# The last four halves of a norm's modulation as multiply-adds on VectorE, the norm chain in front, and fillers on TensorE at the beginning

## The chip, the cores and the metric

One core of a Trainium2 chip runs one layer of a decoder. The metric is device time in microseconds (us) of one execution. The kernel before takes 649.06 us (median of 3 runs, 648.49 to 649.7). The engines are TensorE (PE, with its weight loads PEld), VectorE (DVE), ScalarE (ACT), GpSimd (POOL) and the queue SP, which issues the transfers of the weights.

## The reference, cut to what matters

```python
def rms_norm(x, g):
    y = xf * lax.rsqrt(jnp.mean(xf * xf, axis=-1, keepdims=True) + NORM_EPS)
    return y * g

def modulate(x, g, shift, scale):
    return rms_norm(x, g) * (1.0 + scale[:, None, :]) + shift[:, None, :]

mod = jax.nn.silu(c) @ w_ada[l] + b_ada[l]          # 1 x 6144, from 1024 x 6144 weights
sh1, sc1, g1, sh2, sc2, g2 = jnp.split(mod, 6, axis=-1)
h = modulate(x, norm1_g[l], sh1, sc1)               # 256 x 1024
proj = h @ w_in[l]                                  # 1024 x 3592
...
```

After that come block attention, an mLSTM, an output projection with the gate g1, a second modulated norm (sh2, sc2), a mixture of 32 experts (the routing picks two per token) and a last norm. All is in float32. The change touches only how `sc1` and `sh1` are computed, and the order of the work around them.

## The kernel before, in words

The 256 tokens lie as two tiles of 128. `xt` holds x with tokens on the partitions; TensorE transposes it (`transpose2`, L309) and VectorE and ScalarE copy it out as `xT`, eight blocks k of 128 channels by 256 tokens (`x_evac`, L323). All weights come through a ring of 23 slots of 1 MB (`issue`, `fill`, L135 to L170): SP issues the next chunk when a slot is free, in the order of the list `order`; `done()` gives a slot back, `big()` takes one for a work tile.

The first norm has two parts. `norm1_scale` (L339 to L344) makes 1/rms per token from the sums of squares that ScalarE took; `norm1_rows` (L346) spreads it over the partitions with a matmul as `R1`. The modulation is the product of silu(c) with `w_ada`. Its first 2048 columns (`sh1`: blocks j = 0, 1; `sc1`: blocks j = 2, 3) are used in eight halves of 256 columns, one 1 MB chunk each. `ada_half(j, h)` (L398) computes one half on TensorE, in 8 matmuls with c as the stationary side (L404; the records count 16, two passes each), and VectorE copies the row out of PSUM (L408). `ada_half_cols` (L411) turns it into columns by two tiny matmuls and VectorE adds the bias (L416). Then `mod_a1` (L457) makes (1 + scale) * g, `mod_scale` (L462) multiplies two blocks of `xT` by it and by `R1` on VectorE, and `mod_shift` (L466, L467) adds the shift on ScalarE: once as `hh`, rounded to the matmul's 32-bit form, once back into `xT`. `mod_lo` (L470) makes the rest `hl` = xT - hh on VectorE.

So blocks k = 2m and 2m+1 of h need the halves m of `sc1` and `sh1`, and the loop over m = 0, 1, 2 (L512 on) is a pipeline: in step m TensorE multiplies blocks 2m and 2m+1 with the weights of k, q and v (six calls of `ip`, L489, n = 0 to 5), while the halves for step m+1 are made between them, at n = 2 and n = 4. Each `ip` needs its 128 x 512 weights as a rounded part `whb` (ScalarE, L210) and a rest `wlb` (GpSimd, L211), made by `split_to` into four buffers each, at most three calls ahead; ScalarE may fill a buffer again when TensorE is done with it. I call one such pair of instructions a split.

In all this part each instruction is pinned: `P(...)` and `behind` tie it to the one written before it on its engine, so that the order on an engine is the order of the code. Behind the loop the framework orders the instructions by its own plan. There `mac` (L384) already makes blocks j = 4, 5 and 6 of the modulation on VectorE, one multiply-add per 128 rows of weights, 512 columns wide (L364, L366).

The tile `rowb` holds small parameters, among them the inverse frequencies of the rotary angles (`invf`), which `rope_angles` (L271) reads; ScalarE's queue issues its transfer at the start (L180). `rope_angles` runs in step m = 0 on VectorE, with two sines on ScalarE (L280, L284).

## Time and profile before

| | before |
|---|---|
| median of 3 runs | 649.06 us |
| the profiled execution | 649.01 us |
| its span in the profile | 647.4 us |
| mean granted clock of TensorE | 0.973 of full speed |
| PE, DVE, ACT, POOL busy | 563.3, 170.2, 144.0, 103.7 us |
| weights and data moved | 248.31 MB, mean 384 GB/s |

The span is cut into 40 slices of 16.2 us on the page; a row of digits gives the busy tenths of an engine, PEclk the granted clock in tenths of full speed, GB/s what the transfers moved. Times in the rows below are microseconds from the span's start. A pair "start us, us" is the start and the length; neighbouring instructions of a kind are merged into one row with their count. An idle time in square brackets is that of the engine ahead of the row, with what ended it.

### The profile page before, as it was taken

The page shows a single profiled execution, that of the slowest core. Times are in us where ns is not written, and L with a number is a line of the kernel's source. Part 1 is how long each engine was busy: PE and PEld are TensorE (multiplying, and loading weights), DVE is VectorE, ACT ScalarE, POOL GpSimd, SP SyncE. Part 2 cuts the span into 40 slices and gives each one's busy share as a digit, 9 for nine tenths or more (in the row PEclk, how much of TensorE's full clock was granted, in tenths as well). Part 3 has the DMA queues.
Part 4 walks back from the last instruction along what each step waited for, and adds up shares of the span by engine and source line. Part 5 has one row for each costly group of instructions (what it writes and reads, how often), then busy time and mean ns, then how long its engine had stood idle before and what let it go on. Part 6 is the DMA issues. An engine that isn't in the chain of part 4 may idle for free.

```text
span 647.4 us, 7994 instructions
## 1 busy us (share of the span) xinstructions
PE 563.3 (87%) x3178; PEld 275.3 (43%) x3178; DVE 170.2 (26%) x448; ACT 144.0 (22%) x306; POOL 103.7 (16%) x98
## 2 busy tenths in 40 slices
PE   4899989999997999998889869877988798889874
PEld 3576878875685444352123214211421332233122
DVE  1533979852745030220002002000100110100013
ACT  5453567854443110000000000000000000001013
POOL 2566746672630000000000000000000000000000
PEclk9799999998996999999989999998999999999998
DMA  8999963699696899999999999999999999999994
GB/s 339 423 425 425 415 264 103 245 353 377 220 403 251 330 427 427 427 425 425 428 428 427 425 427 427 429 426 426 426 428 427 426 425 428 425 426 426 428 383 148
DMA packets 41640, 248.31 MB, mean 384 GB/s; under 512 B 4352, under 2 KB 10624, under 8 KB 12928
## 3 DMA queue, kind: packets, MB, share of 16 engines
q1 hardware_dynamic: 41024, 247.00, 92.5%
q10 hardware_dynamic: 576, 0.76, 0.3%
q8 instruction: 26, 0.43, 0.2%
q14 instruction: 14, 0.11, 0.1%
HBM read 246.70 MB, written 1.05 MB: 383 GB/s over the span
## 4 chain that ended last, share of the span: by engine, by line
DMA 50%; PE 36%; DVE 8%; ACT 2%; SPq 2%; issue 1%; DVEq 0%; ACTq 0%
DMA we<-in_wexp_dram 49%; PE f L1124 4%; PE f1a L1103 3%; PE f1b L1103 3%; PE xg_ps L1024 2%; SPq L156 2%; PE adap L404 1%; PE acc L1136 1%; DVE rowb L366 1%; PE xg_ps L1038 1%; DMA xt<-in_x_dram 1%; DVE ropd L563 1%; PE s_ps L637 1%; PE pk L494 1%; PE pk L495 1%
## 5 line engine op out<-in xcount | busy, mean ns | idle before, releaser
L1103 PE MATMUL f1a<-we,xgt 128*32 128x512 f32 x512 | 134.1, 605 | 30.2 <-DMA we<-in_wexp_dram 30.2
L1103 PE MATMUL f1b<-we,xgt 128*32 128x512 f32 x512 | 133.0, 594 | 0.0
L1124 PE MATMUL f<-we,htb 128*32 128x512 f32 (+2 forms) x576 | 82.8, 572 | 17.3 <-DMA we<-in_wexp_dram 17.3
L211 POOL TENSOR_TENSOR wlb<-wi,whb 128x512 fp32r<-128x512 f32 x56 | 74.6, 1349 | 56.4 <-ACT whb L210 48.8
L1103 PEld LDWEIGHTS f1a<-we,xgt 128*32 128x32 f32 x512 | 23.9, 109 | 105.0 <-DMA we<-in_wexp_dram 81.0
L1103 PEld LDWEIGHTS f1b<-we,xgt 128*32 128x32 f32 x512 | 32.7, 109 | 72.6 <-issue 69.8
L1109 ACT ACTIVATE sab<-f1a 128x256 f32<-128x256 f32 x8 | 3.1, 384 | 247.0 <-PE f1a L1103 247.0
L1110 DVE TENSOR_TENSOR acb<-sab,f1a 128x256 f32<-128x256 f32 x8 | 3.4, 422 | 202.6 <-ACT sab L1109 202.6
L1124 PEld LDWEIGHTS f<-we,htb 128*32 128x32 f32 x576 | 21.2, 113 | 64.9 <-DMA we<-in_wexp_dram 31.6
L210 ACT ACTIVATE whb<-wi 128x512 fp32r<-128x512 f32 x56 | 34.5, 632 | 26.8 <-PE pv L497 7.6
L1130 DVE TENSOR_TENSOR ysb<-f,g2b 128x512 f32<-128x512 f32 (+2 forms) x18 | 11.4, 632 | 93.1 <-PE f L1124 93.1
L1024 PEld LDWEIGHTS xg_ps<-gsb,xt 128*128 128x128 f32 x224 | 26.7, 191 | 13.3 <-issue 7.9
L1029 ACT ACTIVATE xgt<-xg_ps,modc,a 128x128 f32<-128x128 f32 x28 | 10.5, 457 | 93.2 <-PE xg_ps L1024 93.2
L1024 PE MATMUL xg_ps<-gsb,xt 128*128 128x128 f32 x224 | 28.6, 279 | 1.9 <-ACT xgt L1029 1.9
L1136 PE MATMUL acc<-ysb,pwb 128*128 128x512 f32 x56 | 27.3, 613 | 2.5 <-DVE ysb L1130 2.3
L211 POOL TENSOR_TENSOR wlb<-wo,whb 128x512 fp32r<-128x512 f32 x16 | 21.0, 1317 | 23.7 <-ACT whb L210 23.2
L366 DVE SCALAR_TENSOR_TENSOR rowb<-wa,cs,rowb 128x512 f32<-128x512 f32 x21 | 23.9, 1139 | 0.3
L506 PE MATMUL pc<-hl,whb 128*128 128x256 f32 x64 | 18.4, 289 | 0.0
L505 PE MATMUL pc<-hh,whb 128*128 128x256 f32 x64 | 18.2, 286 | 0.0
L1136 PEld LDWEIGHTS acc<-ysb,pwb 128*128 128x128 f32 x56 | 9.6, 189 | 19.2 <-issue 8.9
L507 PE MATMUL pc<-hh,wlb 128*128 128x256 f32 x64 | 17.7, 289 | 0.0
L1012 DVE TENSOR_TENSOR gsb<-iot,posm 128x128 f32<-128x128 f32 x16 | 4.4, 289 | 35.7 <-PE xg_ps L1024 32.1
(371 smaller groups left out, 691.5 us busy)
## 6 DMA issues: line engine op xcount, KB each, us to landing
we<-in_wexp_dram SPq DMA_DIRECT2D x188, 1024.0 KB, 19.6
wa<-in_wada_dram SPq DMA_DIRECT2D x24, 1024.0 KB, 13.6
wi<-in_win_dram SPq DMA_DIRECT2D x8, 1024.0 KB, 18.4
wi<-in_win_dram SPq DMA_DIRECT2D x12, 512.0 KB, 14.0
wo<-in_wout_dram SPq DMA_DIRECT2D x4, 1024.0 KB, 7.2
we<-in_wexp_dram SPq DMA_DIRECT2D x4, 512.0 KB, 16.8
we<-in_wexp_dram SPq DMA_DIRECT2D x8, 256.0 KB, 6.3
xt<-in_x_dram SPq DMA_DIRECT2D x1, 1024.0 KB, 5.7
```

What stands on the lines that cost most here:

```text
L156: behind(nc.sync.dma_start(chunks[key][:, 4 * c:4 * (c + n)].rearrange("p (f n) -> p f n", f=4), src[:, :, c:c + n]))
L210: P(A.activation(hi, src, AF.Copy))
L211: G.tensor_tensor(lo, src, hi.bitcast(F32), OP.subtract)
L366: i = V.scalar_tensor_tensor(r, w, cs[:, k:k + 1], r, op0=OP.mult, op1=OP.add)
L505: T.matmul(o, wh[:, cc], hh[:, k], start=k == 0 and c % 2 == 0, stop=False)
L506: T.matmul(o, wh[:, cc], hl[:, k], start=False, stop=False)
L507: T.matmul(o, wl[:, cc], hh[:, k], start=False, stop=k == 7 and c % 2 == 1)
L1024: T.matmul(p[:, (k % 4) * 128:(k % 4 + 1) * 128], xn[:, t, k * 128:(k + 1) * 128], gsb[:, q % 2, t], start=t == 0, stop=t == 1)
L1103: T.matmul(hid[h][CAP * i:CAP * (i + 1), :], xgb[q % 2][:, k, i * CAP:(i + 1) * CAP], w[:, h * 512:(h + 1) * 512], start=k == 0, stop=k == 7)
L1124: m = T.matmul(py[CAP * i:CAP * (i + 1), 0:n], htb[:, f // 2, o:o + CAP], chunks["e", 3 * (4 * q + i) + 2, dh][:, w0:w0 + n], start=f == 0 ...
L1130: V.tensor_tensor(ysb[q % 2][:, c0:c0 + n], py[:, 0:n], g2b[:, c0:c0 + n], OP.mult)
L1136: T.matmul(acc[b], pwb[:, q % 2, t * 128:(t + 1) * 128], ysb[q % 2][:, h * 512:(h + 1) * 512], start=q == 0, stop=q == NQ - 1 - h)
```

## The change

Four things change. The last four halves, for steps m = 1 and m = 2 (`sc1` and `sh1`, halves 2 and 3 of four), are no longer made by TensorE: `ada_half_mac` makes each of them on VectorE in 8 multiply-adds of 256 columns (one TENSOR_SCALAR, seven SCALAR_TENSOR_TENSOR that add to their own result), 4 at each of n = 0 to 3; `ada_mac_cols` turns the row into columns with two tiny matmuls against ones, at n = 4 and n = 5. The halves for step m = 1, made in step m = 0, stay on TensorE. `norm1_scale` moves ahead of the second copy of `xT` and of the first half's copy, and the last two copies of `xT` (on ScalarE) move behind the first `mod_shift`. Of the first splits two instead of three stand ahead of `mod_shift`. TensorE gets transposes of the identity into an unused bank: 28 ahead of x's transposes, then 4, 4 and 8 between the first halves. The transfer of `rowb` moves from ScalarE's queue to SP's, behind the first five chunks.

```diff
@@ -29,6 +29,7 @@
 MLS = (0, 1, 2, 3)
 CT = (3, 5)
 PIN = 24
+WARM = 28
 MACS = (1, 1, 0, 0)
 SLOTS = 23
 KEEP = 9
@@ -120,6 +121,8 @@
         ins = i.ins
         prev = next((x for x in reversed(nc.cur_bb.bb.instructions)
                      if x is not ins and x.engine == ins.engine and x.name not in floating), None)
+        if prev is None:
+            return
         tc.add_manual_dep(ins, prev.name, mybir.DependencyInfo(mybir.DependencyClass.NoSync,
                                                                mybir.DependencyReason.DATA), reason="order")
 
@@ -133,6 +136,8 @@
     keep = [KEEP]
 
     def issue():
+        if nissued[0] == 5:
+            behind(nc.sync.dma_start(rowb[:, 1536:1996], colp[:, 96:556]))
         kind, j, h = order[nissued[0]][:3]
         part = order[nissued[0]][3:]
         if part == (1,):
@@ -177,7 +182,6 @@
 
     nc.sync.dma_start(xt, x.rearrange("(t p) d -> p t d", p=128))
     rowb = big("rowb", [128, 2048])
-    nc.scalar.dma_start(rowb[:, 1536:1996], colp[:, 96:556])
     convw = rowb[:, 1536:1568].rearrange("p (i c) -> p i c", i=4)
     wgate = rowb[:, 1568:1632].rearrange("p (k n) -> p k n", k=8)
     wr = rowb[:, 1632:1920].rearrange("p (k n) -> p k n", k=8)
@@ -314,6 +318,13 @@
     hh = big("hh", [128, 8, S], F32R)
     hl = big("hl", [128, 8, S], F32R)
     pinned[0] = True
+    wp = pA("warm")
+
+    def fillers(n):
+        for _ in range(n):
+            P(T.transpose(wp[:, 0:128], ident, ident))
+
+    fillers(WARM)
     xps = [pacc(f"tp{kk}") for kk in range(4)]
     for kk in range(4):
         transpose2(xt, kk, xps[kk])
@@ -415,6 +426,29 @@
         c0 = 4 * j + 2 * h
         P(V.tensor_tensor(modc[:, c0:c0 + 2], p[:, 256:258], bada[:, c0:c0 + 2], OP.add))
 
+    def ada_half_mac(j, h):
+        r = arow(256)
+        w = chunks["a", j, h].rearrange("p (k n) -> p k n", k=8)
+
+        def run(ks):
+            for k in ks:
+                if k == 0:
+                    P(V.tensor_scalar(r, w[:, k], cs[:, 0:1], None, op0=OP.mult))
+                else:
+                    P(V.scalar_tensor_tensor(r, w[:, k], cs[:, k:k + 1], r, op0=OP.mult, op1=OP.add))
+            if 7 in ks:
+                done()
+
+        return j, h, r, run
+
+    def ada_mac_cols(half):
+        j, h, r, _ = half
+        p = psm("adap")
+        for b in range(2):
+            P(T.matmul(p[:, b:b + 1], r[:, b * 128:(b + 1) * 128], ones[:, 0:1], start=True, stop=True))
+        c0 = 4 * j + 2 * h
+        P(V.tensor_tensor(modc[:, c0:c0 + 2], p[:, 0:2], bada[:, c0:c0 + 2], OP.add))
+
     late = []
 
     def late_rows(j):
@@ -471,19 +505,22 @@
 
     G.memset(wg32, 0.0)
     x_evac(V, 0)
+    norm1_scale()
     x_evac(V, 1)
-    x_evac(A, 2)
-    x_evac(A, 3)
     half = ada_half(2, 0)
-    norm1_scale()
+    fillers(4)
     norm1_rows()
     ada_half_cols(half)
     mod_a1(0)
     half = ada_half(0, 0)
-    ahead()
+    fillers(4)
     mod_scale(0)
+    split_to(2)
     ada_half_cols(half)
+    fillers(8)
     mod_shift(0)
+    x_evac(A, 2)
+    x_evac(A, 3)
 
 
     def ip(p, j, k):
@@ -518,6 +555,21 @@
             rope_tables()
             P(V.tensor_copy(wg32[:, :, 0:8], wgate))
         for n in range(6):
+            if m > 0:
+                if n in (0, 2):
+                    hm = ada_half_mac(2 + j if n == 0 else j, h)
+                    if n == 0:
+                        hs_ = hm
+                if n < 4:
+                    hm[3](range(4 * (n % 2), 4 * (n % 2) + 4))
+                if n == 4:
+                    ada_mac_cols(hs_)
+                    mod_a1(m + 1)
+                    mod_scale(m + 1)
+                if n == 5:
+                    ada_mac_cols(hm)
+                ip((pk, pq, pv)[n // 2], (1, 0, 2)[n // 2], 2 * m + n % 2)
+                continue
             if n == 2:
                 half = ada_half(2 + j, h)
             if n == 4:
```

The order on VectorE around step m = 1 (tile names as in the code: `hl` the rests, `rowb` the row of a half, `wa_0_93` and `wa_0_97` the chunks of a half, `a` the factor, `R` is `R1`). Before:

```order
L470 TENSOR_TENSOR hl<-xT,hh 128x256 x2
L408 COPY rowb<-adap 128x256
L416 TENSOR_TENSOR modc<-adap,colt 128x2
L408 COPY rowb<-adap 128x256
L457 SCALAR_TENSOR_TENSOR a_182<-modc,colt 128x2
L462 SCALAR_TENSOR_TENSOR xT<-xT,a_182,R_179 128x256 x2
L416 TENSOR_TENSOR modc<-adap,colt 128x2
```

And now:

```order
L504 TENSOR_TENSOR hl<-xT,hh 128x256 x2
L436 TENSOR_SCALAR rowb<-wa_0_93,cs 128x256
L438 SCALAR_TENSOR_TENSOR rowb<-wa_0_93,cs,rowb 128x256 x7
L436 TENSOR_SCALAR rowb<-wa_0_97,cs 128x256
L438 SCALAR_TENSOR_TENSOR rowb<-wa_0_97,cs,rowb 128x256 x7
L450 TENSOR_TENSOR modc<-adap,colt 128x2
L491 SCALAR_TENSOR_TENSOR a_211<-modc,colt 128x2
L496 SCALAR_TENSOR_TENSOR xT<-xT,a_211,R_208 128x256 x2
L450 TENSOR_TENSOR modc<-adap,colt 128x2
```

Sixteen multiply-adds stand between the rests of step 1 and the factor that step 2 needs, where two copies out of PSUM stood.

The order on ScalarE behind the first norm (`whb` the rounded weights, `rt` the angles of the rotary tables). Before:

```order
L351 ACTIVATE R_179<-rp 128x256
L210 ACTIVATE whb<-wi_0_82 128x512 x2
L210 ACTIVATE whb<-wi_0_84 128x512
L466 ACTIVATE hh<-xT,modc 128x256
L467 ACTIVATE xT<-xT,modc 128x256
L466 ACTIVATE hh<-xT,modc 128x256
L467 ACTIVATE xT<-xT,modc 128x256
L280 ACT_TABLE_LOAD
L280 ACTIVATE rt<-rt 128x64
L284 ACTIVATE rt<-rt 128x64
L210 ACTIVATE whb<-wi_0_84 128x512
```

And now:

```order
L362 ACTIVATE R_208<-rp 128x256
L214 ACTIVATE whb<-wi_0_81 128x512 x2
L500 ACTIVATE hh<-xT,modc 128x256
L501 ACTIVATE xT<-xT,modc 128x256
L500 ACTIVATE hh<-xT,modc 128x256
L501 ACTIVATE xT<-xT,modc 128x256
L334 ACTIVATE xT<-tp_180 128x512
L334 ACTIVATE xT<-tp_181 128x512
L284 ACT_TABLE_LOAD
L284 ACTIVATE rt<-rt 128x64
L288 ACTIVATE rt<-rt 128x64
L214 ACTIVATE whb<-wi_0_83 128x512 x2
```

The third weight block, with which the product for q begins, is now rounded behind the two sines, and the two copies of `xT` stand between.

The order on TensorE behind the loop, where the gate logits `gp` (L541, now L593) end: blocks 6 and 7 of k and q. Before:

```order
L541 MATMUL gp<-xT,misc 32x256
L497 MATMUL pk_242<-whb,hl 128x512
L497 MATMUL pk_243<-whb,hl 128x512
L494 MATMUL pk_242<-whb,hh 128x512
L495 MATMUL pk_242<-wlb,hh 128x512
L494 MATMUL pk_243<-whb,hh 128x512
L495 MATMUL pk_243<-wlb,hh 128x512
L497 MATMUL pq_244<-whb,hl 128x512
L497 MATMUL pq_245<-whb,hl 128x512
L494 MATMUL pq_244<-whb,hh 128x512
L494 MATMUL pq_245<-whb,hh 128x512
L541 MATMUL gp<-xT,misc 32x256
```

And now:

```order
L593 MATMUL gp<-xT,misc 32x256
L534 MATMUL pk_285<-whb,hl 128x512
L534 MATMUL pk_286<-whb,hl 128x512
L531 MATMUL pk_285<-whb,hh 128x512
L593 MATMUL gp<-xT,misc 32x256
```

Between the last two groups of the gate logits three matmuls stand instead of ten.

## Rows read from the trace of the kernel before

**Rows 1.** The page: granted clock of TensorE and the rate of the transfers in 40 slices of 16.2 us, and the chain that ended last, by engine.

```profile
PEclk9799999998996999999989999998999999999998
GB/s 339 423 425 425 415 264 103 245 353 377 220 403 251 330 427 427 427 425 425 428 428 427 425 427 427 429 426 426 426 428 427 426 425 428 425 426 426 428 383 148
DMA 50%; PE 36%; DVE 8%; ACT 2%; SPq 2%; issue 1%; DVEq 0%; ACTq 0%
```

**Rows 2.** Busy time of the engines by stretch: step m = 1 and step m = 2 (each from its first `hh` to the next step's), and the stretch of the rotary products. Columns: stretch, its length, then busy us and instructions of PE, PEld, DVE, ACT, POOL, then the granted clock, the share of the DMA engines and GB/s.

```profile
33.23:44.42 11.19, 11.19 (x77) 8.18 (x76) 3.18 (x9) 5.41 (x11) 7.53 (x6) 1.00 1.02 424
44.42:57.01 12.59, 12.59 (x90) 8.69 (x89) 3.43 (x9) 5.61 (x12) 8.62 (x7) 1.00 1.01 425
64.00:88.00 24.00, 21.11 (x154) 18.85 (x153) 21.68 (x37) 14.00 (x22) 16.01 (x12) 1.00 0.97 398
```

**Rows 3.** The timeline, start and length: the first `hh` of steps 1, 2 and 3 on ScalarE, and, inside step 1, the second rest, a half on TensorE, and what makes the factor for step 2.

```profile
33.23 0.51 ACT L466 ACTIVATE hh<-xT,modc 128x256 fp32r<-128x256 f32 x1 [0.18 <-DVE modc L416]
...
35.26 0.43 DVE L470 TENSOR_TENSOR hl<-xT,hh 128x256 fp32r<-128x256 f32 x1 [0.52 <-ACT xT L467]
...
36.84 1.07 PE L404 MATMUL adap<-wa,cs 128*32 128x256 f32 x16
...
42.62 0.36 DVE L457 SCALAR_TENSOR_TENSOR a<-modc,colt 128x2 f32<-128x2 f32 x1
...
43.02 0.88 DVE L462 SCALAR_TENSOR_TENSOR xT<-xT,a,R 128x256 f32<-128x256 f32 x2
...
44.17 0.16 DVE L416 TENSOR_TENSOR modc<-adap,colt 128x2 f32<-128x2 f32 x1 [0.27 <-PE adap L414]
...
44.42 0.50 ACT L466 ACTIVATE hh<-xT,modc 128x256 fp32r<-128x256 f32 x1
...
57.01 0.51 ACT L466 ACTIVATE hh<-xT,modc 128x256 fp32r<-128x256 f32 x1 [1.04 <-DVE modc L416]
```

**Rows 4.** VectorE and GpSimd at the same time: the timeline at four places, with an operation of VectorE beside splits on GpSimd, and from the view of a line the shortest, median and longest `mod_scale` in ns.

```profile
15.59 3.90 POOL L211 TENSOR_TENSOR wlb<-wi,whb 128x512 fp32r<-128x512 f32 x3 [11.48 <-ACT whb L210]
...
17.40 2.37 DVE L462 SCALAR_TENSOR_TENSOR xT<-xT,a,R 128x256 f32<-128x256 f32 x2
...
25.91 6.28 POOL L211 TENSOR_TENSOR wlb<-wi,whb 128x512 fp32r<-128x512 f32 x5 [6.41 <-ACT whb L210]
...
31.16 1.05 DVE L457 SCALAR_TENSOR_TENSOR a<-modc,colt 128x2 f32<-128x2 f32 x1
...
70.90 8.06 POOL L211 TENSOR_TENSOR wlb<-wi,whb 128x512 fp32r<-128x512 f32 x5 [2.03 <-DMA wi<-in_win_dram]
...
82.93 4.16 DVE L366 SCALAR_TENSOR_TENSOR rowb<-wa,cs,rowb 128x512 f32<-128x512 f32 x4
...
83.69 1.27 POOL L211 TENSOR_TENSOR wlb<-wi,whb 128x512 fp32r<-128x512 f32 x1 [1.26 <-ACT whb L210]
...
L462 DVE SCALAR_TENSOR_TENSOR xT<-xT,a,R x8: 478/485/1479, 17.4 to 54.9; 128x256 f32<-128x256 f32 x8
```

**Rows 5.** The timeline of the splits in step 1: rounding on ScalarE, with what it waited for, and the rest on GpSimd.

```profile
35.13 1.14 ACT L210 ACTIVATE whb<-wi 128x512 fp32r<-128x512 f32 x2
...
35.83 3.78 POOL L211 TENSOR_TENSOR wlb<-wi,whb 128x512 fp32r<-128x512 f32 x3 [1.41 <-ACT whb L210]
...
40.29 2.68 POOL L211 TENSOR_TENSOR wlb<-wi,whb 128x512 fp32r<-128x512 f32 x2 [0.69 <-ACT whb L210]
...
43.88 0.63 ACT L210 ACTIVATE whb<-wi 128x512 fp32r<-128x512 f32 x1 [2.28 <-PE pv L497]
```

**Rows 6.** The front: the landing of x (a piece of the chain: start, us, what), the timeline of the identity, of the halves and of the first `hh`, of the rounding behind the sines and of q's first product with a rest, and from the view of a line the transposes of x (ns shortest, median, longest, then first and last start).

```profile
1.37 5.73 DMA xt<-in_x_dram
...
1.27 0.30 POOL L235 TENSOR_SCALAR_AFFINE_SELECT ident<-ident 128x128 f32<-128x128 f32 x1
...
L309 PE MATMUL tp<-ident,xt x16: 421/421/445, 7.2 to 10.5; 128*128 128x128 f32 x16
...
10.81 1.19 PE L404 MATMUL adap<-wa,cs 128*32 128x256 f32 x16
...
15.06 1.93 PE L404 MATMUL adap<-wa,cs 128*32 128x256 f32 x16
...
19.88 0.51 ACT L466 ACTIVATE hh<-xT,modc 128x256 fp32r<-128x256 f32 x1 [3.33 <-DVE modc L416]
...
25.21 1.66 ACT L210 ACTIVATE whb<-wi 128x512 fp32r<-128x512 f32 x3
...
26.72 0.39 PE L495 MATMUL pq<-wlb,hh 128*128 128x512 f32 x1
```

**Rows 7.** Busy time and granted clock by stretch (columns as in rows 2): the first slow stretch of TensorE with its neighbours, and a stretch in which it stands idle.

```profile
14.00:14.50 0.50, 0.50 (x6) 0.50 (x5) 0.00 (x0) 0.03 (x1) 0.00 (x0) 1.00 1.02 418
14.50:24.50 10.00, 7.57 (x35) 5.26 (x34) 5.85 (x18) 5.32 (x10) 3.90 (x3) 0.50 1.02 426
...
199.00:201.00 2.00, 0.00 (x0) 0.00 (x0) 1.90 (x20) 1.61 (x4) 0.00 (x0) 0.50 0.99 418
```

**Rows 8.** The timeline behind the loop: the last two groups of the gate logits on TensorE, and their copy on VectorE, with what it waited for.

```profile
60.01 0.62 PE L541 MATMUL gp<-xT,misc 128*32 128x256 f32 x2
...
63.06 0.62 PE L541 MATMUL gp<-xT,misc 128*32 128x256 f32 x2
...
63.72 0.42 DVE L544 COPY gr<-gp 128x256 f32<-128x256 f32 x1 [3.07 <-PE gp L541]
```

## The prediction

> **What bounds the kernel now.** I read the page first: the slices and the chain that ended last [rows 1]. Half of the chain is transfers of expert weights, and from the fifteenth slice (227 us) the rate is about 427 GB/s to the end. Ahead of that it is lower in nearly every slice from the sixth: there the ring is full and SP waits for slots. So the transfers start their last, dense run when the work before it has freed slots, and what the chain of compute loses or gains ahead of 205 us should come out at the end one for one. The change lies in that chain. Next I read the busy times by stretch [rows 2]: in steps m = 1 and 2 TensorE is busy without a gap, VectorE 3.2 and 3.4 us, GpSimd 7.5 and 8.6 us; at first sight TensorE is the bound and VectorE free. In 64 to 88 us VectorE is the bound, 21.68 of 24 us. Then I read the timeline for what ties step to step [rows 3]: a step goes from its first hh to the next step's, 44.42 - 33.23 = 11.19 us and 57.01 - 44.42 = 12.59, together 23.78. Last I looked at what VectorE does while GpSimd makes splits [rows 4].
>
> **The change part by part: steps 1 and 2.** TensorE loses four halves of 1.07 us [rows 3], 4.3 us in all; the two small matmuls for the columns of a half stay. That is the saving if VectorE's chain fits beneath. It has to: in VectorE's new order the sixteen multiply-adds stand behind the two rests of the step and ahead of the factor for the next one. Count the chain from hh to hh. The second rest ends 35.26 + 0.43 - 33.23 = 2.46 us behind hh [rows 3]. A multiply-add of 256 columns does what mod_scale does (two inputs in SBUF, one column of scalars), 0.48 us [rows 4]. Two independent ones took 0.88 [rows 3], but each of ours adds to the one before: the four dependent 512-column ones at 82.93 took 4.16, less the 1.27 of the split that fell among them 0.72 each, about as long as one lasts [rows 4]. So I take the whole 0.48: 16 x 0.48 = 7.7 us. Then the bias of the scale columns 0.16, the factor 0.36, two mod_scale 0.88, the bias of the shift 0.16 [rows 3]: 1.6. The sum is 2.46 + 7.7 + 1.6 = 11.7 us a step with VectorE undisturbed. Two steps give 23.4, against 23.78: even then nearly nothing (-0.4) is won.
>
> It will be disturbed. While a split runs, an operation of VectorE with two inputs in SBUF stands still [rows 4]: the tiny factor at 31.16 took 1.05 us, to 32.21, where the run of five splits ended at 32.19; the two mod_scale at 17.40 took 2.37 instead of 0.88 and ended 0.28 behind the third split (19.49), with 1479 ns for the longer; the four multiply-adds at 82.93 lost about the one split. When both engines have work waiting they alternate. I price a pair: five splits with 512-column operations between took 8.06 us, 1.61 each; three splits with 256-column ones took 3.90, 1.30 each. I take 1.42, nearer to the operation of our width. In a pair one multiply-add is done, so a split costs VectorE 1.42 - 0.48 = 0.94 us. How many fall among the multiply-adds? A step has six. In step 1 before, ScalarE rounds the first two at 35.13, behind the shift, so GpSimd begins at 35.83, about 2.6 us behind hh [rows 5], which is just where the multiply-adds begin. Two or three more follow as TensorE leaves their buffers. With TensorE freed of its halves they come closer together. The sixth waits for a product that now waits for the first eight multiply-adds; it may fall in a gap. I count five: 11.7 + 5 x 0.94 = 16.4 us a step, 32.8 for two, +9.0 over 23.78. Bounds: no split costs anything, -0.4; all six cost their whole 1.27 us, 11.7 + 7.6 = 19.3 a step, +14.8.
>
> What waits behind: the factor, mod_scale, then hh on ScalarE and every product of the next step; TensorE stands idle for some 4 us in each step. The multiply-adds give a chunk's slot back later than TensorE did, but the transfers run at 425 GB/s through these steps [rows 2] and are chunks ahead, so I charge nothing; were that cover gone, one chunk of 1.05 MB is 2.5 us.
>
> By the Trainium skill, page SBUF — State Buffer, section Who interferes with whom, the port pair that VectorE and GpSimd share is held for a whole instruction, and who begins first blocks the other. By that rule a pair would be 1.27 + 0.48 = 1.75, two steps +12.3, and the time 659.5; the three splits at 15.59 lost only 0.09 us to the mod_scale between them [rows 4], so I stay with the rows.
>
> **The front.** The fillers begin when the identity is ready, at 1.57, at the pace of x's transposes, (10.5 - 7.24) / 15 = 0.217 us: 28 take 6.1 and end at 7.7 [rows 6]. x lands at 7.10; without rowb ahead (0.24 MB, 0.55 us at 425 GB/s) perhaps at 6.6, but the fillers hold TensorE. That is +0.5 at the transposes. rowb itself lands behind some 4.8 MB, near 15 us, ahead of its first use behind 21. The clock was granted in full until 14.50 and at half (1.2 of 2.4 GHz) from 14.50 to 24.50, after TensorE had stood idle behind the first half [rows 7]; that half took 1.19 us, the second 1.93 [rows 6]. With the fillers between them I take it as full: the second half about 0.8 shorter, 1/rms out ahead of the copies, two splits ahead of mod_scale instead of three (one split, 1.3). With the +0.5, hh comes at about 18.2 instead of 19.88, a lead of 1.6.
>
> The lead is then lost. The third rounding stood 25.21 - 19.88 = 5.33 us behind hh, behind the table load and the sines, whose angles VectorE computes after the rests [rows 6]. It keeps that distance, but now q's first product needs it and its split: about 18.2 + 5.33 + 0.6 + 1.27 = 25.4 for the product that came at 26.72: lead 1.3. From there GpSimd, with one split more to make and none made ahead, runs without a gap into step 0's factor, which it blocks as it did at 31.16, and into its mod_scale. I charge the front 0 at step 1. Bounds: the lead of 1.3 survives; or TensorE, thinned by the waits, falls to half clock again at q, +1.5 (most of what half clock costs two products, rival C).
>
> **Behind the loop.** In the new order three matmuls instead of ten stand between the last two groups of gate logits; they began 3.05 us apart, 0.27 a matmul without the group's own 0.3 [rows 8], so the second comes 7 x 0.27 = 1.9 earlier. The first came 60.01 - 57.01 = 3.0 behind hh, with v's last product in the way; now hh's 0.5 and eight matmuls stand ahead of it, 2.7, so 0.3 more. VectorE waited 3.07 us for them [rows 8] and is the bound behind [rows 2]. One multiply-add more stands ahead of the rotary products and one fewer behind: nothing. That is -2.2 with TensorE at full clock, 0 with a slow one; I take -1.8.
>
> **Sum.** The profiled execution took 649.01, its span 647.4 and 1.6 around it; the median is 649.06, the same. 649.01 + 9.0 + 0 - 1.8 = 656.2, said as 656. All bounds together: 645.1 to 665.3.
>
> **Rivals.**
> A, the multiply-adds hide: splits slip between them or VectorE has the precedence, the front's lead survives and the logits come early: 649.0 - 0.4 - 1.3 - 2.2 = 645.1. For it: VectorE is idle for eight of eleven us. Against it: the waits of rows 4. It decides on the price of a split: ten of them at 0.22 us or less cancel against the 1.8 and the 0.4. Chance 0.12.
> B, half of it: three splits a step fall among the multiply-adds, 2 x (11.7 + 2.8) = 29.0, +5.3; the lead survives and the logits give 2.2: 650.8. Chance 0.09.
> C, the clock: in its waits TensorE falls to half speed, as it did when it stood idle at 199 us [rows 7], and then runs the next products slowly. The half at 15.06 took 1.93 for the 1.19 at full clock, 0.62 of its length more [rows 6]; the twelve matmuls of two products, 12 x 0.27 = 3.2, would take 2.0 more, once or twice on the path, and the logits not early: 649.0 + 9.0 + 3.0 = 661. Against it: VectorE, not TensorE, sets the step. Chance 0.15.
> D, the fillers start slow: then 28 last 12.2 us, to 13.8, and x's transposes come 6.7 late: some 661. The rows show full clock at 7.24 after 7 us of nothing. Chance 0.02.
> Page TensorE: Matmul & The Clock Gate of the Trainium skill, section What's actually happening, has the half clock as the state without activity; by that D is what would happen, and the trace disagrees.
>
> **How the numbers follow.** Forecast 0.62 (its own range 652 to 660), A 0.12, B 0.09, C 0.15, D 0.02. About 0.2%, 1.3 us, is what a measurement of this kernel can tell from no change. Faster: A and a little of B, 0.13. Same: some of B, 0.06. The rest, 0.81, is slower. The range 648 to 662 leaves out A and the far side of C.
>
> **What would show it.** Right: 256-column multiply-adds of mean length 0.8 to 1.0 us, many at 1.3 or more, ending with splits; from hh to hh about 16 us twice; TensorE idle several us in steps 1 and 2; first hh near 18; the second hh near 33; the gate copy nearer to step 3's hh than 6.7 us. Wrong: multiply-adds near 0.5 us beside splits (A); step 1 begins 1 us or more ahead of 33.23 (the lead survived); a granted clock of 0.50 in steps 1 and 2 with the products as the last wait (C).

## The result, and the profile after

| | before | after |
|---|---|---|
| median beside it on the same chip | 648.77 us (4 runs) | 657.25 us (4 runs, 656.44 to 658.47) |
| ratio, 95% interval | | 1.0123, 1.0098 to 1.0148 |
| profiled execution, span | 649.01, 647.4 us | 658.06, 656.5 us |
| mean granted clock | 0.973 | 0.963 |

The kernel became 1.2% slower. The page of after, which answers to [rows 1]: clock, rate and the chain by engine.

```profile
PEclk9976979999998899999989999999999999999998
GB/s 344 421 426 428 384 220 90 140 320 360 282 359 396 159 426 428 423 428 424 429 426 427 427 426 427 426 427 427 426 427 427 426 427 426 428 423 428 425 398 169
DMA 46%; PE 35%; DVE 11%; ACT 3%; SPq 2%; issue 1%; POOL 0%; DVEq 0%; ACTq 0%
```

VectorE's share of the chain rose from 8 to 11%, and the clock shows a 7 and a 6 in the third and fourth slice, where before had 9. The dense run of transfers starts in the fifteenth slice as before. Now the two late steps by stretch, each from its first `hh` to the next, and the stretch of the rotary products (columns as in [rows 2]).

```profile
30.00:46.07 16.07, 11.29 (x43) 8.28 (x42) 13.86 (x23) 5.50 (x10) 8.51 (x7) 0.79 1.02 424
46.07:62.21 16.14, 11.54 (x44) 8.98 (x43) 13.94 (x23) 5.61 (x10) 8.58 (x7) 0.79 1.01 425
70.00:94.00 24.00, 21.86 (x136) 18.47 (x135) 21.32 (x38) 12.09 (x22) 16.45 (x11) 0.91 0.67 257
```

A step takes 16.07 and 16.14 us where it took 11.19 and 12.59 [rows 2]; VectorE, busy for 3.2 and 3.4 us of a step before, is busy for 13.9 of 16.1 us, and TensorE, busy without a gap before, stands idle for 4.7 us. The timeline of the first of these steps, the answer to [rows 3 and 5]:

```profile
30.00 0.51 ACT L500 ACTIVATE hh<-xT,modc 128x256 fp32r<-128x256 f32 x1 [0.52 <-DVE modc L427]
...
32.60 6.96 POOL L215 TENSOR_TENSOR wlb<-wi,whb 128x512 fp32r<-128x512 f32 x5 [1.55 <-ACT whb L214]
32.76 8.12 DVE L438 SCALAR_TENSOR_TENSOR rowb<-wa,cs,rowb 128x256 f32<-128x256 f32 x7
...
41.18 3.61 DVE L438 SCALAR_TENSOR_TENSOR rowb<-wa,cs,rowb 128x256 f32<-128x256 f32 x7
...
45.09 0.88 DVE L496 SCALAR_TENSOR_TENSOR xT<-xT,a,R 128x256 f32<-128x256 f32 x2
45.57 1.55 POOL L215 TENSOR_TENSOR wlb<-wi,whb 128x512 fp32r<-128x512 f32 x1 [6.01 <-ACT whb L214]
46.07 0.51 ACT L500 ACTIVATE hh<-xT,modc 128x256 fp32r<-128x256 f32 x1 [0.58 <-DVE modc L450]
```

The seven multiply-adds beside five splits take 8.12 us, the seven without a split 3.61. The chain of waits shows the same one by one (start, us, what), and the view of waits shows who stands behind them (us, times, longest):

```profile
32.76 1.43 DVE rowb L438
...
34.21 1.41 DVE rowb L438
...
35.65 1.40 DVE rowb L438
...
37.07 1.38 DVE rowb L438
...
38.47 1.38 DVE rowb L438
...
39.87 0.50 DVE rowb L438
```

```profile
PE adap L448 <- DVE rowb L438: 9.1, 2, 4.6
```

While the five splits run, one multiply-add gets done per split, every 1.4 us; when they end (39.56), each takes 0.50. TensorE waits 9.1 us in the two steps for the finished rows. The front, which answers to [rows 6]:

```profile
1.62 6.24 PE L325 MATMUL warm<-ident 128*128 128x128 f32 x28 [1.62 <-POOL ident L239]
...
7.65 1.96 PE L313 MATMUL tp<-ident,xt 128*128 128x128 f32 x16
...
9.65 1.07 PE L415 MATMUL adap<-wa,cs 128*32 128x256 f32 x16
...
12.23 1.07 PE L415 MATMUL adap<-wa,cs 128*32 128x256 f32 x16
...
15.70 0.51 ACT L500 ACTIVATE hh<-xT,modc 128x256 fp32r<-128x256 f32 x1 [1.36 <-DVE modc L427]
...
21.03 2.17 ACT L214 ACTIVATE whb<-wi 128x512 fp32r<-128x512 f32 x4
...
23.05 0.50 PE L532 MATMUL pq<-wlb,hh 128*128 128x512 f32 x1 [0.85 <-POOL wlb L215]
```

The first `hh` comes 4.18 us earlier than before, q's first product with a rest 3.67, the next step's `hh` (30.00 for 33.23) 3.23. Behind the loop, for [rows 8]:

```profile
64.68 1.57 PE L593 MATMUL gp<-xT,misc 128*32 128x256 f32 x12
...
68.23 0.62 PE L593 MATMUL gp<-xT,misc 128*32 128x256 f32 x2
...
69.67 0.62 PE L593 MATMUL gp<-xT,misc 128*32 128x256 f32 x2
...
70.33 0.42 DVE L596 COPY gr<-gp 128x256 f32<-128x256 f32 x1 [5.67 <-PE gp L593]
```

```profile
38.70:45.20 6.50, 4.02 (x12) 2.97 (x12) 6.11 (x14) 0.34 (x1) 0.86 (x1) 0.50 1.04 433
55.70:65.60 9.90, 8.36 (x30) 5.80 (x32) 6.94 (x18) 3.19 (x6) 1.58 (x2) 0.50 1.01 427
```

The last two groups of the logits now stand 1.44 us apart instead of 3.05, as the order promised, but the copy comes 8.12 us behind the step's `hh` at 62.21; before it was 6.71. The stretches at half clock (1.2 of 2.4 GHz), each begun while TensorE stood idle, say part of the reason.

The table below adds up every kernel of this study from five landmarks of its trace: the first `hh` of steps 1 and 3, the gate copy `gr`, the first sum into `cat` of attention (145.08 in before), and the end. The clock is the granted one between `gr` and `cat`.

| kernel | hh of step 1 | two steps | to gr | gr to cat (clock) | cat to end | span | median |
|---|---|---|---|---|---|---|---|
| before | 33.23 | 23.78 | 6.71 | 81.36 (1.00) | 502.3 | 647.4 | 649.0 |
| after | 30.00 | 32.21 | 8.12 | 84.61 (0.96) | 501.6 | 656.5 | 657.25 |
| e1_front | 29.61 | 23.77 | 6.71 | 81.33 (1.00) | 501.3 | 642.7 | 646.04 |
| e2_macs | 32.76 | 34.21 | 4.50 | 81.89 (1.00) | 501.5 | 654.9 | 658.94 |
| e3_psum | 31.14 | 23.72 | 7.07 | 81.90 (1.00) | 501.6 | 645.4 | 645.91 |
| e4_nowarm | 31.94 | 24.07 | 6.71 | 85.00 (0.94) | 501.5 | 649.2 | 649.07 |
| e5_warmonly | 29.44 | 23.75 | 6.71 | 83.47 (0.96) | 500.8 | 644.2 | 645.66 |
| e6_nosplit | 29.65 | 24.14 | 4.95 | 83.10 (0.98) | 501.5 | 643.3 | 646.71 |
| e7_keepclock | 29.38 | 34.18 | 6.75 | 83.45 (0.96) | 501.2 | 655.0 | 656.53 |
| e8_hybrid | 29.53 | 22.02 | 6.71 | 83.51 (0.96) | 500.4 | 642.2 | 644.67 |
| e9_beforewarm | 32.01 | 24.00 | 6.71 | 81.35 (1.00) | 501.4 | 645.5 | 648.95 |
| e10_hybridmin | 29.58 | 22.01 | 6.71 | 81.36 (1.00) | 502.3 | 642.0 | 644.96 |

From before to after: -3.2 in the front, +8.4 in the two steps, +1.4 to `gr`, +3.25 to `cat`, -0.7 behind, together +9.1. Each row is one execution, and its time can lie some way from the median: e2's took 656.54 us, e4's 651.66. The median of before is the one beside e1, e2, e3 and e6.

### The profile page after: what moved, and what is told of

It is laid out like the page before. It is cut to its first block, busy times and chain, and to the rows that moved or that the text cites. A ratio compares the mean times of both kernels' runs of the same rounds, so it can differ in the third digit from the quotient of the medians.

```text
span 656.5 us, 7984 instructions
## 1 busy us (share of the span) xinstructions
PE 570.7 (87%) x3158; PEld 281.4 (43%) x3158; DVE 189.8 (29%) x476; ACT 144.2 (22%) x306; POOL 106.9 (16%) x98
## 3 DMA queue, kind: packets, MB, share of 16 engines
HBM read 246.70 MB, written 1.05 MB: 377 GB/s over the span
## 4 chain that ended last, share of the span: by engine, by line
DMA 46%; PE 35%; DVE 11%; ACT 3%; SPq 2%; issue 1%; POOL 0%; DVEq 0%; ACTq 0%
DMA we<-in_wexp_dram 46%; PE f L1176 5%; DVE rowb L438 3%; PE f1a L1155 3%; PE f1b L1155 3%; PE xg_ps L1076 3%; PE acc L1188 2%; SPq L161 2%; PE s_ps L689 1%; PE xg_ps L1090 1%; PE pc L543 1%; DMA xt<-in_x_dram 1%; PE pc L544 1%; PE pc L542 1%; DVE ropd L615 1%
## 5 line engine op out<-in xcount | busy, mean ns | idle before, releaser
L1155 PE MATMUL f1a<-we,xgt 128*32 128x512 f32 x512 | 132.5, 606 | 29.3 <-DMA we<-in_wexp_dram 29.3
L1155 PE MATMUL f1b<-we,xgt 128*32 128x512 f32 x512 | 131.4, 594 | 0.0
L1176 PE MATMUL f<-we,htb 128*32 128x512 f32 (+2 forms) x576 | 83.1, 572 | 17.5 <-DMA we<-in_wexp_dram 17.4
L215 POOL TENSOR_TENSOR wlb<-wi,whb 128x512 fp32r<-128x512 f32 x56 | 77.7, 1408 | 63.1 <-ACT whb L214 60.3
L215 POOL TENSOR_TENSOR wlb<-wo,whb 128x512 fp32r<-128x512 f32 x16 | 21.0, 1313 | 23.7 <-ACT whb L214 22.7
L438 DVE SCALAR_TENSOR_TENSOR rowb<-wa,cs,rowb 128x256 f32<-128x256 f32 x28 | 22.6, 807 | 1.0
## 6 DMA issues: line engine op xcount, KB each, us to landing
wi<-in_win_dram SPq DMA_DIRECT2D x8, 1024.0 KB, 16.2
```

The source lines that it names most:

```text
L215: G.tensor_tensor(lo, src, hi.bitcast(F32), OP.subtract)
L438: P(V.scalar_tensor_tensor(r, w[:, k], cs[:, k:k + 1], r, op0=OP.mult, op1=OP.add))
L1155: T.matmul(hid[h][CAP * i:CAP * (i + 1), :], xgb[q % 2][:, k, i * CAP:(i + 1) * CAP], w[:, h * 512:(h + 1) * 512], start=k == 0, stop=k == 7)
L1176: m = T.matmul(py[CAP * i:CAP * (i + 1), 0:n], htb[:, f // 2, o:o + CAP], chunks["e", 3 * (4 * q + i) + 2, dh][:, w0:w0 + n], start=f == 0 ...
```

## The experiments

My theory: what costs is the multiply-adds, because VectorE with two inputs in SBUF takes turns with GpSimd's splits. Rivals: the dependent chain is slow whatever stands beside it; TensorE's clock; something in the front.

**e1_front: the front without the multiply-adds.** The branch `if m > 0:` of the loop is taken out.

> The changed kernel with its front (28 + 4 + 4 + 8 fillers, norm chain first, two splits and the row tables' load moved), but with the four late halves back on TensorE as in the kernel before. Theory: the front alone is worth the lead that the trace of after shows at hh2 (30.00 against 33.23 us), and the two steps cost 24 us again: hh6 near 54.0, and the end 2.5 to 3.5 us earlier than before, about 645.5 to 646.5 us. Rival, the prediction's own term (the front's lead is lost by the end): 648.8 us, within 0.2% of before. Rival, the order of the plan behind the loop costs something with this front too: 647.5 us or more, with hh6 near 54 all the same.

Measured 646.04 us against 649.04, ratio 0.9950 (0.9925 to 0.9976). The steps are back at 23.77 us and the front's lead, 3.62 us, arrives at `gr` undiminished. So the front is a gain by itself, and after's loss is all behind it.

**e2_macs: the multiply-adds with the old front.** The functions `ada_half_mac` and `ada_mac_cols` and the branch of the loop, put into the kernel before.

> The kernel before with its own front (no fillers, x's copies in the old order, table load on ScalarE's queue), and only the four late halves as multiply-adds on VectorE. Theory: the two steps take 16.1 us each from hh2 at 33.2, hh6 stands near 65.4, and what is lost behind it (1.4 us to gr, some 3 us further down) is lost too: about 661 us, 1.8% slower than before. Rival: the loss behind the loop comes from the new front (its order of loads), not from the multiply-adds: 657 us. Rival, the multiply-adds cost less where they start later against the splits: below 655 us.

Measured 658.94 us, ratio 1.0143 (1.0109 to 1.0178), between the theory's 661 and the first rival's 657; the trace divides it. The theory's steps are there, and dearer: 17.1 us each, not 16.1. Its losses behind the loop are not: `gr` came 4.50 behind `hh`, not 8.12, and nothing like 3 us was lost up to `cat`. So the multiply-adds cost their time in the steps under either front, and the losses behind are no fixed part of them. The profiled execution is the fastest of six, though; the others took 658.80 to 660.07 us, and where they lost the rest no trace shows. Timeline:

```profile
47.85 1.92 DVE L485 SCALAR_TENSOR_TENSOR xT<-xT,a,R 128x256 f32<-128x256 f32 x2
47.97 1.52 POOL L211 TENSOR_TENSOR wlb<-wi,whb 128x512 fp32r<-128x512 f32 x1 [5.66 <-ACT whb L210]
...
66.80 1.06 PE L579 MATMUL gp<-xT,misc 128*32 128x256 f32 x12
```

Here the sixth split falls upon `mod_scale`, which takes 1.92 instead of 0.88; that is the 1.0 by which the step is dearer. It holds up `hh` but not TensorE, so some 1.0 of what `gr` seems to gain behind `hh` is the same time, counted in the step. In after it began at 45.57, when `mod_scale` was already running, and took 1.55 itself while `mod_scale` kept its 0.88. `mod_scale` and the logits' start (66.80, 0.17 ahead of the step's `hh` at 66.97) show the rest: TensorE had its clock back by then, 1.06 for the twelve matmuls that took 1.57 in after.

**e3_psum: the running sum in PSUM.** The same sixteen multiply-adds, but each reads one operand from SBUF and one from PSUM; the last one writes the row to SBUF.

```diff
-        r = arow(256)
+        p = psm("adap")
+        r, o = p[:, 128:384], arow(256)
...
-                    P(V.scalar_tensor_tensor(r, w[:, k], cs[:, k:k + 1], r, op0=OP.mult, op1=OP.add))
+                    P(V.scalar_tensor_tensor(o if k == 7 else r, w[:, k], cs[:, k:k + 1], r, op0=OP.mult, op1=OP.add))
```

> The changed kernel with the running sum of each late half in a PSUM tile instead of the SBUF row (the last multiply-add writes the row to SBUF), so that VectorE reads one operand from SBUF and one from PSUM. Theory (a multiply-add with two SBUF operands loses its time to POOL's split, which has two as well): seven multiply-adds take 3.6 to 4.3 us beside the splits instead of 8.1, a step from hh to hh takes 11.5 to 13 us, POOL's splits about 0.5 to 1.2 us each instead of 1.39, and the end is 647 to 651 us. Rival (the long dependent chain costs by itself, the splits have no part in it): seven take 8 us as before, 657 us. Rival (a PSUM operand is slower on VectorE than an SBUF one): a multiply-add over 0.6 us, in which case the step keeps 14 us or more.

Measured 645.91 us, ratio 0.9945 (0.9919 to 0.9972): 11 us faster than after. The line's view (ns shortest, median, longest), then the timeline beside the splits:

```profile
L439 DVE SCALAR_TENSOR_TENSOR adap<-wa,cs,adap x24: 487/490/491, 34.0 to 52.6; 128x256 f32<-128x256 f32 x24
```

```profile
33.72 6.29 POOL L215 TENSOR_TENSOR wlb<-wi,whb 128x512 fp32r<-128x512 f32 x5 [1.11 <-ACT whb L214]
...
34.01 3.12 DVE L439 SCALAR_TENSOR_TENSOR adap<-wa,cs,adap 128x256 f32<-128x256 f32 x6
```

Five splits run beside them, and not one multiply-add is longer than 491 ns, where after's run from 484 to 1421; the splits take 1.26 each instead of 1.39. A step takes 11.86 us, against the 11.7 that I had counted for an undisturbed one. The two steps, 23.72, are no shorter than e1's 23.77: VectorE's chain alone is about as long as what TensorE took with its four halves. Both rivals fall: neither the dependence nor the PSUM operand costs anything to speak of. Two other stretches of this execution were slow: step 0 ran at 0.57 from 24 to 28 us, and the first `hh` of step 1 came 1.14 later than after's with the same front; and behind a wait of 1.98 us in step 2 TensorE was at 0.50 from 56 to 58, with `gr` 7.07 behind `hh`. By the Trainium skill, page SBUF — State Buffer, section Who interferes with whom, an instruction of VectorE with two SBUF inputs contends with GpSimd's reads and one with at most one, outside the two-port modes, does not; by that, the trace agrees on both sides.

**e6_nosplit: after without the splits of the two steps.** GpSimd's rests of twelve weight blocks are left out; TensorE multiplies with those of earlier blocks instead.

```diff
-            G.tensor_tensor(lo, src, hi.bitcast(F32), OP.subtract)
+            if not 8 <= i < 20:
+                G.tensor_tensor(lo, src, hi.bitcast(F32), OP.subtract)
```

> The changed kernel without POOL's splits of the twelve chunks of the two late steps (the low halves wlb that TensorE reads there are those of earlier chunks; left out: the low part of these weights). Theory (VectorE's multiply-adds and POOL's splits take turns): all multiply-adds take 0.50 us, the seven in front 3.5 us instead of 8.1, a step 11.5 to 12 us from hh to hh, and the end about 648 us. Rival (the chain is slow by itself): the seven still take 8 us, the step 16 us and the end 657 us. Rival (the step is bound by ScalarE's rests, which wait for TensorE): the multiply-adds get fast and the step stays over 14 us.

Measured 646.71 us, ratio 0.9956 (0.9925 to 0.9986). The multiply-adds, untouched in SBUF, are all short:

```profile
L439 DVE SCALAR_TENSOR_TENSOR rowb<-wa,cs,rowb x28: 483/485/487, 32.4 to 51.0; 128x256 f32<-128x256 f32 x28
```

The first step took 11.55 us, as the theory had it, the second 12.59, since a split made for the work behind the loop (51.91) fell upon `mod_scale`, 1.92 us for 0.88. With e3 this settles the cause of the 8.4 us from both sides: take the second SBUF operand away or take the splits away, and the steps are back at 23.7 to 24.1 us.

**e7_keepclock: fillers where TensorE waits in the two steps.** In after, `ada_mac_cols(hs_, 36)` and `ada_mac_cols(hm, 14)`, with

```diff
+        for _ in range(n):
+            P(T.transpose(p[:, 128:256], ident, ident))
```

> The changed kernel with 36 transpositions of the unit matrix on TensorE ahead of the first columns in each late step, and 14 ahead of the second, where TensorE waits for VectorE's row; they write an unused part of the same PSUM tile. Theory (the 1.4 us lost behind the loop, and perhaps 0.3 us in each step, are TensorE's clock, which falls while it waits): the granted clock stays at 1.00 from 36 to 66 us, gr stands 6.7 us behind the last rest instead of 8.1, the steps still take 15.5 to 16.1 us, and the end is 654.5 to 656. Rival (the clock has no part; the 1.4 us are the order of the instructions): 657.3 us, gr 8.1 us behind. Rival (the fillers stand in the way of the columns): 658 us or more.

Measured 656.53 us, ratio 1.0114 (1.0099 to 1.0129): no difference from after that could be told. The clock held at 1.00 from 36 to 44 us, not through to 66 (0.88 and 0.69 up to 52), and the steps became longer, 17.2 and 17.0:

```profile
40.60 4.71 DVE L438 SCALAR_TENSOR_TENSOR rowb<-wa,cs,rowb 128x256 f32<-128x256 f32 x7
...
43.25 1.26 POOL L215 TENSOR_TENSOR wlb<-wi,whb 128x512 fp32r<-128x512 f32 x1 [4.27 <-ACT whb L214]
```

With TensorE quick, v's product gives its buffer back earlier (ScalarE rounds at 42.54 instead of 44.86), and the sixth split falls among the second seven multiply-adds, 4.71 us for 3.61; in the next step it falls upon the factor, 1.05 us for 0.16. What the clock gave, the next collision took. `gr` stood 6.75 behind `hh`, as the theory said, but the plan behind the loop had also changed (the groups of logits 3.02 us apart again), so this run alone doesn't price the clock there; e6, with after's own order, does it better (below).

**e4_nowarm, e5_warmonly, e9_beforewarm: the parts of the front.** e4 is e1 with `WARM = 0`; e5 is e1 without the lines `fillers(4)`, `fillers(4)`, `fillers(8)`; e9 is the kernel before with `fillers(28)` alone.

> The kernel of e1_front (new front, late halves on TensorE) without its 28 fillers ahead of x's transpositions; those of 4, 4 and 8 further down stay. Theory (the fillers raise TensorE's clock before x lands, although the record reads 1.00 there without them too): x's sixteen transpositions take 3.6 us again instead of 1.96, the first rest hh0 stands at 16.5 to 17.5 us instead of 15.3, and the end is 1 to 2 us later than e1_front's 646.0: 647 to 648. Rival, by which my forecast priced them at nothing (the clock is up at the start in any case): transpositions still 2 us, hh0 at 15.3, 646 us.

> The kernel of e1_front without the fillers of 4, 4 and 8 in the norm chain's waits; the first 28 stay. Theory (the first 28 and the order of the norm chain make the gain): hh0 at 15.3 us, hh2 at 29.6 to 30.5, the end within 1 us of e1_front, 645.5 to 647. Rival (TensorE's clock falls in the gaps of the norm chain without them): the products rp and adap and the columns between 10 and 15 us at half pace, hh0 0.5 to 1.5 us later, the first step's pk and pq at half pace too, 647 to 649 us.

> The kernel before with nothing added but the 28 fillers ahead of x's transpositions. Theory (in e4_nowarm the new order of the front without these fillers gained nothing by the end, so the fillers carry the gain): the sixteen transpositions take 1.96 us instead of 3.65, the halves' products that took 1.93 us at half pace take 1.07, hh0 stands at 17 to 18.3 us instead of 19.88, and the end is 645.5 to 647.5. Rival (fillers and order are both needed: with the old order TensorE waits for the norm chain behind the halves in any case): hh0 at 19 us or later, the end within 1 us of before, 648 to 649.5.

Measured: e4 649.07 us, ratio 0.9986 (0.9957 to 1.0014); e5 645.66, 0.9949 (0.9932 to 0.9965); e9 648.95, 0.9989 (0.9972 to 1.0006). So the later sixteen fillers are worth nothing beside the 28, and of the rest neither the 28 fillers alone nor the new order alone (with the sixteen) shows a gain in time; both together give 3 us. The traces say a little more: each part alone brings `gr` to 62.72, 1.0 us ahead of before (63.72), and both together bring it to 60.09. e4 was expected 1 to 2 us behind e1, and is 3 behind; e9 was expected to gain, and by its time the rival holds, though its first `hh`, at 18.57, is earlier than the rival said. The line views of x's transposes in e4 and in e1, then the stretches of e4, e9 and e1 in which the clocks differ:

```profile
L313 PE MATMUL tp<-ident,xt x16: 421/421/447, 6.6 to 9.9; 128*128 128x128 f32 x16
```

```profile
L313 PE MATMUL tp<-ident,xt x16: 272/273/328, 6.7 to 8.4; 128*128 128x128 f32 x16
```

```profile
24.00:28.00 4.00, 3.98 (x10) 3.13 (x11) 0.00 (x0) 0.81 (x2) 4.00 (x4) 0.57 1.04 429
```

```profile
14.00:24.00 10.00, 7.32 (x32) 5.11 (x24) 6.50 (x20) 4.97 (x11) 3.90 (x3) 0.50 1.02 424
```

```profile
14.00:24.00 10.00, 7.01 (x44) 4.66 (x44) 5.71 (x23) 6.78 (x13) 5.00 (x5) 1.00 1.02 423
```

e4's first `hh` stands at 16.67, only 1.36 behind e1's 15.31, but its step 0 runs at 0.57 from 24 to 28 us and `hh` of step 1 is 2.33 behind. In e9 the norm chain still stands behind the copies, and the clock is at half from 14 to 24. Such a fall does not come in every execution: e4's twelve lie from 646.73 to 651.98, and the profiled one, with a second fall at 88 to 92 us, is at 651.66. That the others differ by the same falls is likely, but not shown. Nor do the 28 fillers and the new order rule the fall out: e3 has both and its step 0 ran at 0.57 too.

**e8_hybrid and e10_hybridmin: the better version.** The new front; of each late step's halves the first on VectorE with the sum in PSUM, the second on TensorE. e10 leaves out the fillers of 4, 4 and 8.

```diff
+            if n == 0 and m > 0:
+                half = ada_half_mac(2 + j, h)
+                half[3](range(8))
-            if n == 2:
+            if n == 2 and m == 0:
                 half = ada_half(2 + j, h)
             if n == 4:
-                ada_half_cols(half)
+                (ada_mac_cols if m > 0 else ada_half_cols)(half)
```

> Meant to beat both kernels: the new front; of each late step's two halves the first (the scale's, needed early) as multiply-adds on VectorE with the running sum in PSUM, the second on TensorE. Theory (TensorE sets the step in e1_front, and eight products of a half, some 1.0 us, go from it; eight multiply-adds of 0.52 us end before pq's product does): a step takes 10.2 to 11.5 us from hh to hh, hh6 stands at 51 to 52.5 us instead of 53.4, and the end is 644 to 645.5 us. Rival (the row is ready no earlier than TensorE would have made it, or POOL's splits get slower): steps as in e1_front, 646 us. Rival (the gain is lost behind the loop): hh6 earlier, end 646.

> The kernel of e8_hybrid without the fillers of 4, 4 and 8, which in e5_warmonly were worth nothing. Theory (the gains of e5_warmonly and e8_hybrid add up, since they lie in different stages): 644 to 645 us, within 0.5 us of e8_hybrid's 644.7, steps from hh to hh of 10.4 and 11.6 us. Rival (the first step is slower without them, since TensorE's clock falls between 14 and 20 us): 645.5 to 646.5 us, with hh2 0.5 to 1 us later than e8_hybrid's 29.53.

Measured 644.67 us, ratio 0.9936 (0.9923 to 0.9949), and 644.96, 0.9929 (0.9912 to 0.9945): both beat both kernels. Timeline of e8 in step 1:

```profile
35.57 0.48 DVE L439 SCALAR_TENSOR_TENSOR rowb<-wa,cs,adap 128x256 f32<-128x256 f32 x1
...
36.19 0.58 PE L448 MATMUL adap<-ones,rowb 128*128 128x1 f32 x4 [0.26 <-DVE rowb L439]
36.70 1.07 PE L415 MATMUL adap<-wa,cs 128*32 128x256 f32 x16
```

The row is ready at 36.05, 0.26 us behind TensorE's last product for q. The two steps take 22.0 us, 1.8 less than with all halves on TensorE, near the two halves of 1.07 that TensorE lost. Over e1 the medians show 1.1 to 1.4 us, and the intervals overlap, so this last step rests on the traces more than on the times.

## Why the prediction was right or wrong

The time was forecast at 656.0 with 652 to 660 as its own range, and it is 657.25. That is one term right and several that were wrong and nearly cancel.

**Steps 1 and 2: right, +9.0 forecast, +8.4 found.** Each piece can be read off: the second rest ends 2.45 us behind `hh` (2.46 forecast); sixteen multiply-adds last 12.4 us (7.7 + 4.7 = 12.4); a multiply-add beside a split takes 1.38 to 1.43 (pair priced 1.42); five splits fall among them and the sixth costs VectorE nothing, as counted; the tail is 1.3 instead of 1.6, as the factor took 0.16 and not 0.36. e3 and e6 show the mechanism, and e3's 11.86 the undisturbed step of 11.7. Rivals A and B fall with it. The rule of the whole instruction, 1.75 a pair, was too dear by 0.35; which parts of the two overlap no run here shows.

**The front: wrong, 0 forecast, -3.2 found.** Two steps failed. The first is "a lead of 1.6". It was 4.18, because x's transposes took 1.96 us instead of 3.65 and the norm chain moved further ahead than I counted: from the first half to the second it is 2.58 us instead of 4.25 [rows 6]. I had read the granted clock of 1.00 ahead of 14.50 [rows 7] as full speed; it was the pace of 421 ns a transpose [rows 6] that told the truth, against 272 here. So D was right in its mechanism and wrong in its price: the fillers do start slow, at the 0.22 us that I took for full pace, and save x's transposes from it. The Trainium skill, page TensorE: Matmul & The Clock Gate, section What's actually happening, has the half clock as the state without activity; I wrote that the trace disagrees, and by e4 and e1 the trace agrees. The second step that failed is "the lead is then lost". Its mechanism is there: the rounding stands 21.03 - 15.70 = 5.33 us behind `hh`, to the hundredth as forecast, and q waits 0.85 for its split. But it takes 0.95 of the lead and not all of it: from the first `hh` to that of step 1 it is 14.30 us for 13.35.

**Behind the loop: wrong, -1.8 forecast, +1.4 found.** Two steps failed. The first is "TensorE at full clock". In after TensorE was at half clock until 65.6; e6 has the same order and was at full clock in this place. From the last two matmuls for the columns to v's last product it is 0.84 us in after and 0.44 in e6, from there to the gate logits 2.84 and 1.57, from there to k's product 1.50 and 0.98: together 2.2 us. Behind that both need the same, 4.15 and 4.14. This is rival C's mechanism, 2.2 where I priced it at 2.0, at one place; it did not set the steps, as I had argued.

The second step that failed is "now hh's 0.5 and eight matmuls stand ahead of it". Before, the first twelve matmuls of the logits ran ahead of the step's `hh` (57.01). Now they stand behind v's last product, which itself waits for the last multiply-adds. The line of before, then v's last product in after, then e6:

```profile
55.18 1.06 PE L541 MATMUL gp<-xT,misc 128*32 128x256 f32 x12
```

```profile
61.84 0.77 PE L531 MATMUL pv<-whb,hh 128*128 128x512 f32 x1
```

```profile
51.77 1.92 DVE L497 SCALAR_TENSOR_TENSOR xT<-xT,a,R 128x256 f32<-128x256 f32 x2
...
52.05 0.48 PE L532 MATMUL pv<-whb,hh 128*128 128x512 f32 x1
...
53.62 1.06 PE L594 MATMUL gp<-xT,misc 128*32 128x256 f32 x12
```

In e6 `gr` stands 4.95 behind `hh`, but `hh` came 1.04 late by the split upon `mod_scale`, for which TensorE did not wait. Without that it would be 6.0 by my estimate, and after without its 2.2 of slow clock 5.9. So at full clock the new order is worth 0.7 to 0.8 us and not 2.2, and -0.8 + 2.2 is the +1.4 found.

**Further down: not forecast, +2.5 found.** I took what `gr` has lost to come out at the end one for one. From `gr` to `cat` after needs 3.25 us more. The table divides it: kernels with all late halves as multiply-adds and clock 1.00 need 81.9, those with clock 1.00 otherwise 81.35, so 0.55 is the plan's other order; the other 2.7 us go with a granted clock of 0.96 there. The stretches of after and of e2 (columns as in [rows 2]):

```profile
70.33:154.94 84.61, 82.47 (x519) 68.62 (x519) 65.61 (x131) 56.22 (x116) 54.02 (x41) 0.96 0.62 232
```

```profile
71.47:153.36 81.89, 79.78 (x521) 67.16 (x521) 65.59 (x131) 56.66 (x117) 54.44 (x41) 1.00 0.63 233
```

Every execution under 1.00 in that stretch lies between 83.1 and 85.0, after and others alike. So this part is rather a fall of the clock in that execution than a cost of the change, though three more executions of after, 656.44 to 658.47, don't say how often it comes. Why the clock fell there stays open.

So the sum, +9.0 + 0 - 1.8 = +7.2, met a span that grew by 9.1: the front's error (-3.2) is outweighed by the logits (+3.2) and by the stretch behind (+2.5), less 0.6 in the steps.

## What to carry to other kernels

Before work is moved to an engine that looks idle, ask with whom its operand reads collide: sixteen multiply-adds with two SBUF operands cost 4.2 us a step beside GpSimd's two-operand splits, and the same ones with the running sum in PSUM cost nothing. They win nothing either, since the chain of all sixteen is as long as the step. Give the idle engine the part that is needed first and is done in time (one half of two, not both), so that the engine that sets the step gets shorter. And read a clock by the duration of a known instruction in that place: a short burst of harmless work ahead of the first real product can be worth microseconds, but only if the chain behind it can use them.

## What the hardware showed that I had not expected

The granted clock reads 1.00 in stretches where the engine is at half pace: in e4's 7 to 11 us it stands at 1.00 with transposes of 421 ns, in e1 at 1.00 with 272 ns. That the record begins at full until its first event is my reading; no run shows it.

TensorE's clock differs between the profiled executions in places where the kernels are alike: in the stretch from `gr` to `cat` a granted clock of 0.94 to 0.98 goes with 1.2 to 3.7 us more than 1.00 does. Whether it also makes the spread between executions of one kernel (5.3 us in e4) is not shown, since there is one trace of each.

The place of a single split decides some 1.0 us a step: upon `mod_scale` in e2 and e6, among the multiply-adds or upon the factor in e7, at no cost to VectorE in after. An engine made faster (TensorE by its fillers in e7) moved it into the way. The same delay can then look like a gain further on, as `gr` behind a late `hh` did in e2 and e6.
